# First stream column loaded ahead of the last conditioning weights, and conditioning units moved along the stream of a hybrid decoder step

## The chip, the cores and the metric

The kernel runs on one core of one Trainium2 chip. The metric is the device time of one execution in microseconds (us). Three runs of the kernel before took 1305.91, 1309.7 and 1313.38 us; their median is 1309.7 us.

## What is computed

One layer of a decoder, for 512 prompt rows and 8 single sample rows of width 1024, all in f32:

```python
mod = (c @ w_ada + b_ada)[:, None, :]                 # conditioning: 9 vectors c -> 6 * 1024 columns
sh1, sc1, gt1, sh2, sc2, gt2 = jnp.split(mod, N_MOD, axis=-1)
h = _rmsnorm(x, norm1_g) * (1.0 + sc1) + sh1
proj = h @ w_in                                       # 8768 columns for both mixers
...                                                   # A) sparse attention on q, k, v; B) gated delta rule
mixed = (gate_a * o_nsa + gate_b * o_dn) @ w_out
x = x + gt1 * mixed
h = _rmsnorm(x, norm2_g) * (1.0 + sc2) + sh2
x = x + gt2 * (jnp.square(jax.nn.relu(h @ w_up)) @ w_down)
```

In mixer B a chunk of 128 rows needs the inverse of a triangular matrix per head (the triangular stage), and then a recurrence goes over the four chunks: each chunk's state comes out of the one before. The outputs are the new rows, the caches and the states.

## The kernel before

All work is put into the queues of the engines by one Python program; a scheduling pass then orders each engine's instructions with a simulated timeline, in which work with a higher priority goes first when it is ready. On the chip every engine runs its own list in order and waits on semaphores.

**Conditioning.** `c @ w_ada` is cut into 24 units of 256 columns (`ada`, line 256). A unit has two loads of 512 KB (`ada_load`, line 245, issued by SyncE), 16 matmuls in four row groups into a bank `ek` (line 169), a copy `ma` on ScalarE (line 261), a second small product (line 266, recorded under line 153) and an add on VectorE (line 267). The first 8 units, for the first norm, run at the start (lines 767 to 784): `fetch(n)` issues the loads of the units up to n, seven are issued by the time that j is 3, and the eighth at j = 4. Of their loads all but two go into the pool `q4`, and two into the ring `wraw` of four buffers (`NRAW`). The list `starts` chains these loads: each is issued after the one before it on SyncE.

**Stream.** Everything else that multiplies by weights is a list of units, each 128 columns of `w_in`, later of `w_out`, `w_up` and `w_down`. A unit's weights (`w_load`, line 348, 512 KB, the ring `wraw` again) are split into a rounded part `wh` (ScalarE, line 397, or VectorE, line 399, by kind) and a rest `wl` (VectorE, line 401), and three products are summed (line 153): 48 matmuls in two halves of the rows, each half in one of two banks `pg`. The input is split likewise into `hh` and `hl` by `modulate` (lines 308 to 336), which gives the input in four quarters of two blocks each; a quarter needs two conditioning units. `load_upto` issues loads in the order of the list, about two units ahead; the first stream column is issued by `load_upto(0)` at line 785, chained behind the last of `starts`.

The units' order is written out by hand: the columns for the compressed keys, the gates and mixer B (lines 724 to 734), and then the string `FILL` (line 37), in which `a` is one of the other 16 conditioning units, `q` a query column, `ks` and `kw` two key columns each, `ma` and `mb` the merge gates and `z` the output gate of mixer B. A conditioning unit of `FILL` has both its loads in the ring `wraw`. A `q` may be put down only when the recurrence has finished a chunk (`gate`); its result goes where the triangular matrices `LU` were.

**What runs beside it.** Generators for the triangular stage (`triangular`), the recurrence, the sample rows and the attention put their instructions down between the stream's units, at due times counted in TensorE time of the stream (`run`, line 474), with a higher priority. The last part of the triangular stage is a sequence of small matmuls (32 and 64 wide) with evictions by VectorE and ScalarE. The recurrence begins with `pre1` (line 1139): a scaled transposed key and the decay matrix, whose operand `grhs` is made on VectorE and ScalarE (lines 1001 and 999), multiplied on TensorE and put through an exponential (line 1004). `pre2` (line 1151) is the next product. The sample rows' convolution state `sr` is loaded in eight pieces on ScalarE's queue (line 1286). In the attention the value products use the banks `ek` too (line 1500).

Of the kernel before, what the change touches and what calls it, by code (L numbers as in the profile page):

```python
# [33 lines left out]
ON_B = "vector"  # L34
ON_A = "vector"
WLP = 0
FILL = "a a a a a q ks a a q q kw q a q q q ma ma ma q a z mb a ma z mb ma z mb a z ma mb a ma z a mb ma z a mb a a z z mb mb"
R1 = 5
R2 = 10
R3 = 6.4  # L40
# [29 lines left out]
def hybrid_step(ctx: ExitStack, tc: tile.TileContext, A, O, dbg=None):  # L70


    nc = tc.nc
# [19 lines left out]
    def kb4(pool, shape, dt, name, tag, bufs=None):  # L93
        x = pool.tile([128, 2 * SLOT], dt, name=name, tag=tag, **({} if bufs is None else dict(bufs=bufs)))
        n = 1
        for v in shape:
            n *= v
        x = x[:, 0:n]
        return x if len(shape) == 1 else x.rearrange("p (a b) -> p a b", a=shape[0])
# [79 lines left out]
    for hf in range(2):  # L179
        c = slice(hf * 512, hf * 512 + 512)  # L180
        nc.sync.dma_start(crow[hf][0:1], A["c_prompt"][:, c])
        starts = [nc.sync.dma_start(crow[hf][1:9], A["c_sample"][:, c])]
# [62 lines left out]
    def ada_load(j0, hf, pool=None):  # L245
        if pool is None:
            wa = kb4(wp, (4, 256,), F32, "wa", "wraw", bufs=NRAW)
        else:
            wa = kb4(pool, (4, 256,), F32, "wa", "q4")
        with tc.issue_after(starts[-1].ins) if len(starts) < 17 else nullcontext():  # L250
            r = nc.sync.dma_start(wa, w_ada[:, hf * 4:hf * 4 + 4, j0 * 256:j0 * 256 + 256])
        if len(starts) < 17:
            starts.append(r)
        return wa

    def ada(j0, wa):

        pa = bank("ek")
        quarters(pa[:, 0:256], lambda j, s: cT[:, 18 * j + 9 * s:18 * j + 9 * s + 32], lambda j, s: wa[j // 2][:, j % 2 * 2 + s], True, True, 2)
        ma = e2("ma")[:, 0:256]  # L260
        nc.scalar.copy(out=ma, in_=pa[:, 0:256])

        def rest():
            pt = bank("ek")
            for hf in range(2):
                mm(pt[:, hf * 16:hf * 16 + 9], ma[:, hf * 128:hf * 128 + 128], sel, start=True, stop=True)
            nc.vector.tensor_tensor(mod[:, 2 * j0:2 * j0 + 2], pt[:, 0:32].rearrange("p (b n) -> p b n", b=2)[:, :, 0:9],  # L267
                                    vec[:, 16 + 2 * j0:18 + 2 * j0, None].to_broadcast([128, 2, 9]), op=ALU.add)
        return rest
# [27 lines left out]
    def norm1(t):  # L297
        n = x_rows(t)[1]
        xt = x_tile(t)
        nc.vector.tensor_scalar(xt[0:n], xt[0:n], ssq[0:n, t:t + 1], None, op0=ALU.mult)  # L300
        for hf in range(2):
            x_transposed(xnT, xt[:, hf * 512:(hf + 1) * 512], t, hf * 4, "sc" if hf else "pt")
# [38 lines left out]
    pos = {"unit": 0, "half": 0, "split": 0, "load": 0}  # L341
# [6 lines left out]
    def w_load(ap):  # L348
        def load():
            raw = kb4(wp, (KT, 128,), F32, "raw", "wraw", bufs=NRAW)  # L350
            nc.sync.dma_start(raw, ap)
            return raw
        return load

# [18 lines left out]
    def load_upto(g):  # L373
        while pos["load"] <= min(g, len(groups) - 1):
            x = groups[pos["load"]]
            with tc.issue_after(starts[-1].ins) if pos["load"] == 0 else nullcontext():
                x.raw = x.load()
            pos["load"] += 1

    def split_upto(u):  # L380
        while pos["split"] <= u and pos["split"] < len(units):
            un = units[pos["split"]]
            if "ada" in un and pos["split"] > pos["unit"]:
                return
            load_upto(un["g"])
            if un.get("same"):
                un["w"] = un["same"]["w"]
            elif "ada" not in un:
                raw = groups[un["g"]].raw
                if un.get("keep"):  # L390
                    wh, wl = (kb4(wp, (KT, 128,), F32R, "wk", "wkeep", bufs=NKEEP) for _ in range(2))
                else:
                    wh = kb4(wp, (KT, 128,), F32R, "wh", "wh")
                    wl = kb4(wp, (KT, 128,), F32R, "wl", "wl")
                if un["on"] == "scalar":
                    with tc.issue_after(slot["mixed"].ins) if un.get("keep") else nullcontext():
                        nc.scalar.copy(out=wh, in_=raw)  # L397
                else:
                    (nc.vector if un["on"] == "vector" else nc.gpsimd).tensor_copy(wh, raw)
                kp = KT - WLP  # L400
                nc.vector.tensor_tensor(wl[:, 0:kp], raw[:, 0:kp], f32(wh[:, 0:kp]), op=ALU.subtract)  # L401
                if WLP:
                    nc.gpsimd.tensor_tensor(wl[:, kp:], raw[:, kp:], f32(wh[:, kp:]), op=ALU.subtract)
                un["w"] = wh, wl
                load_upto(un["g"] + 2)
            pos["split"] += 1
# [9 lines left out]
    def step():  # L416
# [7 lines left out]
        if "ada" in un:  # L424
            split_upto(pos["unit"])
            rest = ada(un["ada"], [x.raw for x in groups[un["g"] - 1:un["g"] + 1]])
            load_upto(un["g"] + 2)

            def ev():
                yield  # L430
                yield
                rest()
            e = ev()
            next(e)
            live.append(("ada", e))
            pos["unit"] += 1
            if pos["unit"] < len(units):
                split_upto(pos["unit"])
            return True
# [306 lines left out]
    nxt = {"a": 8, "q": 0, "ma": 0, "z": 0, "mb": 0}  # L746
    for x in FILL.split():
        if x in nxt:
# [11 lines left out]
    def fetch(n):  # L760

        for j in range(len(was), n):
            i = j // 2 + 4 * (j % 2)
            was[i] = [ada_load(i, 0, q4), ada_load(i, 1, None if j % 4 == 3 else q4)]
# [4 lines left out]
    for j in range(8):  # L769
        if j < 5:  # L770
            norm1(j)
        i = j // 2 + 4 * (j % 2)
        rest.append(ada(i, was[i]))
        fetch(j + 4 if j < 5 else 8)
        if j % 2:
            for r in rest:
                r()
            rest = []
            if j < 4:
                continue  # L780
            for i in range(j // 2 if j > 5 else 0, j // 2 + 1):
                modulate(xnT, 0, 0, 8, hh, hl, 2 * i, 2 * i + 2)
            if j == 5:
                slot["early"] = slot["rest"]
# [1215 lines left out]
```

## Time and profile before

| | |
|---|---|
| median of three runs | 1309.7 us |
| the profiled execution | 1307.84 us |
| its span, first to last instruction | 1306.1 us |
| mean granted TensorE clock | 0.969 |
| TensorE, VectorE, ScalarE, GpSimd busy | 93%, 65%, 50%, 18% |
| DMA | 149.82 MB, mean 115 GB/s |

The engines are PE (TensorE), PEld (its weight loads), DVE (VectorE), ACT (ScalarE), POOL (GpSimd) and SP (SyncE); a q behind the name is its queue of DMA issues. A timeline row has the start, the duration, the engine, the line, the operation, the tiles (out, then in) and the count, and in brackets how long the engine was idle before and what ended that. Line 153 is the helper through which nearly all matmuls go, so the tile names tell them apart: `bpg` is the stream, `bek` and `bsp` are the other banks. Most of the span belongs to the stream; the conditioning stands at the start, ahead of the recurrence near 350 us, and in single units up to 812 us.

### The profile page before, as it was taken

To read this page: it belongs to the slowest core of one execution; us is meant where nothing else is said; L and a number is where in the kernel's file an instruction comes from. 1 tells how busy PE (TensorE), PEld (TensorE's weight loads), DVE (VectorE), ACT (ScalarE), POOL (GpSimd) and SP (SyncE) were. 2 spreads that over 40 slices of the span, in tenths; PEclk is the share of its full clock that TensorE was granted. 3 is DMA by queue.
4 is the path that set the end of the run, shared out by engine and by line. 5 is a ranking of instruction groups with operands and counts; after the bars stand their busy time and mean duration, and the time that the engine had idled before them with its cause. 6 is when DMAs were issued, how large, how long until landed. Compare 5 with 4: busy or idle time off the path is not lost. (4 is left out here: it accounts for less than half of the span.)

```text
span 1306.1 us, 26716 instructions
## 1 busy us (share of the span) xinstructions
PE 1216.6 (93%) x10356; PEld 1150.1 (88%) x10356; DVE 843.8 (65%) x2291; ACT 647.2 (50%) x1561; POOL 230.1 (18%) x323
## 2 busy tenths in 40 slices
PE   4899899999888999799998899999999999999997
PEld 3788889989788999678887798989999999999996
DVE  4576958795357788787777787896834334334355
ACT  4565857654243336656646677574643132232244
POOL 2112100112111111312221323230431021020000
PEclk9899989999699999899999899999999999999999
DMA  8852412425613345346344222371732332332533
GB/s 273 216 156 74 126 32 51 119 78 151 182 47 108 103 130 146 98 116 197 99 116 136 74 72 85 94 196 33 210 95 69 98 95 83 97 97 83 161 90 105
DMA packets 234834, 149.82 MB, mean 115 GB/s; under 512 B 9290, under 2 KB 230018, under 8 KB 234444
## 3 DMA queue, kind: packets, MB, share of 16 engines
q1 hardware_dynamic: 224804, 134.77, 36.4%
q0 software_dynamic: 2240, 6.38, 1.8%
q10 hardware_dynamic: 7664, 6.97, 1.8%
q8 instruction: 81, 1.33, 0.4%
q14 instruction: 45, 0.37, 0.1%
HBM read 136.87 MB, written 15.60 MB: 117 GB/s over the span
## 5 line engine op out<-in xcount | busy, mean ns | idle before, releaser
L153 PE MATMUL bpg<-hh,wh 128*128 128x256 f32 (+1 forms) x1168 | 342.2, 293 | 1.2 <-ACT hh L1521 0.7
L153 PE MATMUL bpg<-hh,wl 128*128 128x256 f32 (+1 forms) x1168 | 337.5, 289 | 2.0 <-DVE wl L401 2.0
L153 PE MATMUL bpg<-hl,wh 128*128 128x256 f32 (+1 forms) x1168 | 337.7, 289 | 0.0
L153 PEld LDWEIGHTS bpg<-hh,wh 128*128 128x128 f32 x1168 | 225.2, 193 | 5.2 <-issue 2.0
L153 PEld LDWEIGHTS bpg<-hh,wl 128*128 128x128 f32 x1168 | 224.5, 192 | 4.0 <-DVE wl L401 2.5
L153 PEld LDWEIGHTS bpg<-hl,wh 128*128 128x128 f32 x1168 | 225.5, 193 | 1.5 <-issue 0.8
L401 DVE TENSOR_TENSOR wl<-raw,wh 128x1024 fp32r<-128x1024 f32 x149 | 183.0, 1229 | 65.7 <-ACT wh L397 60.3
L397 ACT CAST wh<-raw 128x1024 fp32r<-128x1024 f32 x117 | 121.6, 1048 | 181.9 <-PE bpg L153 174.5
L153 PE MATMUL bpg<-act,wh 128*128 128x264 f32 (+1 forms) x1024 | 186.5, 284 | 0.0
L153 PEld LDWEIGHTS bpg<-act,wh 128*128 128x128 f32 x1024 | 157.7, 188 | 0.1
L153 PE MATMUL bpg<-act,wl 128*128 128x264 f32 (+1 forms) x512 | 145.0, 284 | 0.2 <-DVE wl L401 0.2
L153 PE MATMUL bpg<-h2h,wh 128*128 128x256 f32 (+1 forms) x448 | 126.7, 283 | 0.0
L153 PE MATMUL bpg<-h2h,wl 128*128 128x256 f32 (+1 forms) x448 | 126.6, 282 | 0.0
L153 PE MATMUL bpg<-h2l,wh 128*128 128x256 f32 (+1 forms) x448 | 126.3, 282 | 0.0
L1848 POOL TENSOR_TENSOR r<-r 128x520 f32<-128x520 f32 (+2 forms) x40 | 54.1, 1354 | 291.2 <-ACT r L1847 291.2
L1811 DVE SCALAR_TENSOR_TENSOR o_dn<-bpg,consts,o_dn 128x256 f32<-128x256 f32 x80 | 38.3, 484 | 100.3 <-PE bpg L153 100.3
L153 PEld LDWEIGHTS bpg<-act,wl 128*128 128x128 f32 x512 | 96.5, 189 | 0.5 <-DVE wl L401 0.4
L153 PEld LDWEIGHTS bpg<-h2h,wl 128*128 128x128 f32 x448 | 84.4, 188 | 0.3 <-DVE wl L401 0.2
L153 PEld LDWEIGHTS bpg<-h2l,wh 128*128 128x128 f32 x448 | 84.4, 188 | 0.0
L153 PEld LDWEIGHTS bpg<-h2h,wh 128*128 128x128 f32 x448 | 84.3, 188 | 0.0
L153 PE MATMUL bsp<-K,qst 128*128 128x288 f32 (+6 forms) x288 | 68.9, 317 | 5.5 <-DVE consts L267 2.3
L1851 DVE TENSOR_TENSOR act<-r,act 128x520 fp32r<-128x520 f32 (+2 forms) x40 | 23.6, 590 | 73.4 <-ACT act L1850 73.3
(634 smaller groups left out, 2453.3 us busy)
## 6 DMA issues: line engine op xcount, KB each, us to landing
raw<-in_w_in SPq DMA_DIRECT2D x68, 512.0 KB
wa<-in_w_ada SPq DMA_DIRECT2D x48, 512.0 KB
raw<-in_w_down SPq DMA_DIRECT2D x40, 512.0 KB
raw<-in_w_up SPq DMA_DIRECT2D x36, 512.0 KB
raw<-in_w_out SPq DMA_DIRECT2D x12, 512.0 KB
Sx<-in_state_dn SPq DMA_DIRECT2D x16, 256.0 KB
out_s_dn<-Sx SPq DMA_DIRECT2D x16, 256.0 KB
pg<-in_cache_k_slc SPq DMA_DIRECT2D x16, 128.0 KB
```

Source lines behind the costliest of these rows:

```text
L153: nc.tensor.matmul(out, lhs, rhs, start=start, stop=stop)
L397: nc.scalar.copy(out=wh, in_=raw)
L401: nc.vector.tensor_tensor(wl[:, 0:kp], raw[:, 0:kp], f32(wh[:, 0:kp]), op=ALU.subtract)
L1811: nc.vector.scalar_tensor_tensor(xi[:, q], p[:, 0:n], mod[:, m + i, 0:1], xi[:, q], op0=ALU.mult, op1=ALU.add)
L1848: nc.gpsimd.tensor_tensor(r, r, r, op=ALU.mult)
L1851: nc.vector.tensor_tensor(b_, r, f32(a), op=ALU.subtract)
```

## The change

It has two parts. The first stream column is issued by `load_upto(0)` when j is 3, that is behind the fourteenth conditioning load and ahead of the last two, and it is a link of the chain `starts`, so that the last two are issued after it. In `FILL` three conditioning units move: five units ahead of the first `q` become three, two behind `ks` become one, and the three come again behind the sixth `q`, behind the third `mb` and, with the last ones spread, between the last `z`.

```diff
--- before.py
+++ after.py
@@ -34,7 +34,7 @@
 ON_B = "vector"
 ON_A = "vector"
 WLP = 0
-FILL = "a a a a a q ks a a q q kw q a q q q ma ma ma q a z mb a ma z mb ma z mb a z ma mb a ma z a mb ma z a mb a a z z mb mb"
+FILL = "a a a q ks a q q kw q a q q q a ma ma ma q a z mb a ma z mb a ma z mb a z ma mb a ma z a mb ma z a mb a z a z a mb mb"
 R1 = 5
 R2 = 10
 R3 = 6.4
@@ -348,7 +348,10 @@
     def w_load(ap):
         def load():
             raw = kb4(wp, (KT, 128,), F32, "raw", "wraw", bufs=NRAW)
-            nc.sync.dma_start(raw, ap)
+            with tc.issue_after(starts[-1].ins) if pos["load"] == 0 else nullcontext():
+                r = nc.sync.dma_start(raw, ap)
+            if pos["load"] == 0:
+                starts[-1] = r
             return raw
         return load
 
@@ -373,8 +376,7 @@
     def load_upto(g):
         while pos["load"] <= min(g, len(groups) - 1):
             x = groups[pos["load"]]
-            with tc.issue_after(starts[-1].ins) if pos["load"] == 0 else nullcontext():
-                x.raw = x.load()
+            x.raw = x.load()
             pos["load"] += 1
 
     def split_upto(u):
@@ -772,6 +774,8 @@
         i = j // 2 + 4 * (j % 2)
         rest.append(ada(i, was[i]))
         fetch(j + 4 if j < 5 else 8)
+        if j == 3:
+            load_upto(0)
         if j % 2:
             for r in rest:
                 r()
```

## Rows read from the trace of the kernel before

**Rows 1.** The page, part 1: busy time, share of the span, instructions.

```profile
PE 1216.6 (93%) x10356; PEld 1150.1 (88%) x10356; DVE 843.8 (65%) x2291; ACT 647.2 (50%) x1561; POOL 230.1 (18%) x323
```

**Rows 2.** The chain that ended last, its longest piece: start, us, what.

```profile
946.57 303.91 PE bpg L153 x2529
```

**Rows 3.** Windows of 25 us: busy PE, PEld, DVE, ACT, POOL; clock; DMA share; GB/s.

```profile
350.00:375.00 25.00, 18.86 (x120) 18.07 (x120) 12.84 (x32) 7.42 (x20) 2.77 (x3) 0.80 0.57 161
...
400.00:425.00 25.00, 25.00 (x237) 22.96 (x237) 20.45 (x54) 8.76 (x22) 2.66 (x2) 1.00 0.54 148
...
725.00:750.00 25.00, 19.75 (x130) 16.95 (x129) 17.63 (x62) 17.57 (x51) 7.98 (x18) 0.80 0.24 65
```

**Rows 4.** Windows ahead of the recurrence, columns as above.

```profile
336.00:342.00 6.00, 6.00 (x131) 5.29 (x130) 2.68 (x6) 0.59 (x1) 0.00 (x0) 0.50 0.49 166
...
349.60:353.60 4.00, 0.02 (x4) 0.03 (x1) 3.33 (x6) 2.96 (x8) 0.00 (x0) 0.77 0.71 164
...
353.60:358.00 4.40, 4.40 (x18) 4.21 (x19) 0.84 (x2) 0.60 (x1) 1.28 (x1) 0.50 1.05 347
```

**Rows 5.** Timeline of the start, several engines: start, us, engine, line, operation, [idle before <-releaser].

```profile
32.95 4.01 SPq L351 DMA_DIRECT2D raw<-in_w_in  x2
...
35.85 1.07 PE L169 MATMUL bek<-wa,consts 128*32 128x256 f32 x16 [1.10 <-DMA wa<-in_w_ada]
...
39.82 1.94 PE L169 MATMUL bek<-wa,consts 128*32 128x256 f32 x16 [2.90 <-DMA wa<-in_w_ada]
...
42.10 1.05 ACT L397 CAST wh<-raw 128x1024 fp32r<-128x1024 f32 x1
...
43.41 0.56 PE L153 MATMUL bpg<-hh,wh 128*128 128x256 f32 x1
...
48.26 0.17 DVE L336 TENSOR_TENSOR hl<-xnT,hh 128x16 fp32r<-128x16 f32 x1
```

**Rows 6.** Timeline of PE ahead of and into the recurrence.

```profile
341.34 1.94 PE L169 MATMUL bek<-wa,consts 128*32 128x256 f32 x16
...
347.15 1.14 PE L153 MATMUL bsp<-iv,TA 64*64 64x64 f32 x30
...
348.54 1.07 PE L169 MATMUL bek<-wa,consts 128*32 128x256 f32 x16
...
353.60 1.19 PE L153 MATMUL bsp<-grhs,rounded 128*128 128x512 f32 x2 [3.98 <-DVE consts L267]
...
354.59 0.41 PE L153 MATMUL bpg<-hh,wh 128*128 128x256 f32 x1
...
356.72 0.86 PE L153 MATMUL bek<-consts,ma 128*128 128x9 f32 x4
...
365.77 0.41 PE L153 MATMUL bsp<-qT,kT 128*128 128x128 f32 x2
```

**Rows 7.** Timeline of SP's queue in the same stretch.

```profile
327.26 0.92 SPq L251 DMA_DIRECT2D wa<-in_w_ada  x2
...
343.30 6.46 SPq L351 DMA_DIRECT2D raw<-in_w_in  x3
```

**Rows 8.** Timelines of DVE and ACT in the same stretch.

```profile
347.41 0.69 DVE L399 CAST wh<-raw 128x1024 fp32r<-128x1024 f32 x1 [4.93 <-DMA raw<-in_w_in]
...
349.12 1.04 ACT L397 CAST wh<-raw 128x1024 fp32r<-128x1024 f32 x1 [3.31 <-DMA raw<-in_w_in]
...
352.77 0.68 DVE L1001 TENSOR_TENSOR grhs<-rounded,gsp 128x512 fp32r<-128x512 f32 x1
...
354.83 7.61 ACTq L1286 DMA_DIRECT2D sr<-in_state_conv  x8
```

**Rows 9.** Timeline of PE later: a conditioning unit, its second product, a wait.

```profile
411.90 1.07 PE L169 MATMUL bek<-wa,consts 128*32 128x256 f32 x16
...
423.05 0.51 PE L153 MATMUL bek<-consts,ma 128*128 128x9 f32 x4
...
735.56 0.50 PE L153 MATMUL bsp<-K,qst 128*128 128x288 f32 x2 [2.28 <-DVE consts L267]
```

## The prediction

> **What bounds the kernel now.** I read the page's table of engines first. TensorE is busy for 93% of the span, VectorE for 65%, ScalarE for 50% [rows 1]. The chain of waits, followed back from the end, is 303.91 us of TensorE without a break from 946.57 us on: 2529 matmuls, 0.12 us each [rows 2]. So whatever reaches that point earlier ends earlier by as much, and the question is only when TensorE gets there. The table by windows shows where it loses time before that: 18.86 of 25 us busy at 350 to 375 at a clock of 0.80, 25.00 of 25 at 400 to 425, 19.75 of 25 at 725 to 750 [rows 3]. The loss at 350 is the place that the change touches. Inside it TensorE does next to nothing for 4.0 us (349.60 to 353.60), and then runs at a granted clock of 0.50, that is 1.2 GHz, from 353.60 [rows 4]. The timelines of the single engines tell why.
>
> **Part one, the load order at the start.** Three weight columns matter here. In the kernel before, SyncE issues the first two stream columns at 32.95, after all sixteen loads of the first eight conditioning units [rows 5]. The matmuls of the seventh unit's last load begin at 35.85, those of the eighth at 39.82, and both waited for their loads, so two loads of 512 KB take 39.82 - 35.85 = 3.97, about 2.0 us each. The first column is cast from 42.10, the second follows, and the stream begins at 43.41 [rows 5]. The change puts the first column ahead of the last two conditioning loads, issues no DMA more, and passes no other queue. So the column lands about 4 us earlier, and each of the two loads that it passes 2.0 us later.
> What this is worth: TensorE stands idle from 36.92 (35.85 + 1.07) to 39.82, 2.90 us. At best the cast begins at 42.10 - 3.97 = 38.13, its 1.05 us end at 39.2, and stream matmuls fill the gap 0.6 us before the eighth unit would have begun: -0.6. At worst TensorE's queue still has the eighth unit first, and all behind it is 2.0 us later: +2.0. The eighth unit also feeds the last quarter of the normalised input, whose last piece is written at 48.26, 4.85 us after the stream begins [rows 5]; that piece gets later too, while the 36 matmuls that don't need it take between 36 x 0.12 = 4.3 us and, at the doubled step of the slow clock, 8.6 us, so they cover it nearly. Between -0.6 and +2.0 I take 0: the row nearest to the deciding one is the 2.90 us gap, which is there either way, and the work on TensorE is the same.
>
> **Part two, two conditioning units fewer ahead of the recurrence.** Five units stand there before (the fourth begins at 341.34, the fifth at 348.54), three after. Their weights share a ring of four buffers with the stream columns, so the columns behind them are issued only as the units free buffers: the three columns after the five units go out at 343.30, right after the fourth unit (341.34 + 1.94 = 343.28) [rows 6, 7]. They land late: VectorE waits 4.93 us for one until 347.41, ScalarE 3.31 us for the next until 349.12, and both engines are in order, so what the recurrence's first decay product needs stands behind these casts and is made only at 352.77 + 0.68 = 353.45 [rows 8]. TensorE begins that product at 353.60 after 3.98 us idle, and the page's name for the releaser, a conditioning add, is only the piece that came last [rows 6].
> After the change the ring holds the columns two units earlier in its order. The load pair that goes out at 327.26 [rows 7], when the second unit is through, is then the first two of these three columns. Landing as late after issue as before (347.41 - 343.30 = 4.1), they are there at 331.4, long before the casts are due. So the wait of 3.98 us goes, and so does the work of the two units, 1.94 and 1.07. Both ends: if only the wait goes, -4.0; if TensorE runs straight on from its last small matmul (347.15 + 1.14 = 348.29), the two units gone as well, -(3.98 + 1.94 + 1.07) = -7.0. Late next is the eviction of these small matmuls on VectorE and ScalarE, in order ahead of the decay operand; it will take some of it back. I take the middle, **-5.5**.
> Behind that product nothing more is gained. The next recurrence product begins at 365.77, and ahead of it stand transposes of a small state whose eight loads ScalarE issues from 354.83 for 7.61 us, right behind the decay's exponential [rows 6, 8]. That chain moves as a whole with the product at 353.60. The stream column that runs beside it from 354.59 at the slow clock (18 matmuls of all kinds in 4.40 us [rows 4]), and the two small conditioning products (0.86 us at 356.72 is one of two) are hidden under it: 0. It could be -2 if the state's loads gain by having fewer weight loads beside them, DMA share 1.05 there [rows 4], or +1.
> The Trainium skill, Perfetto Trace Analysis, section Matmul Optimizations, speaks against this: the matmul engine scales with its use, so matmuls should run back to back, and the two units did fill the triangular stage. The row says that they don't keep the clock up: at 336 to 342 TensorE is busy 6.00 of 6.00 us and is granted 0.50 [rows 4]. By the rule the sum would be that of the clock rival below; by the row it stays.
>
> **Part three, where the units go.** Behind the recurrence's first columns stood two units, the first at 411.90; now there is one. A unit costs 1.07 plus 0.51 for its second product [rows 9], 1.6 us at full clock. TensorE is full there (25.00 of 25 [rows 3]), so -1.6. Further on, in the attention stretch, three units come in: +4.8 if TensorE is full at each, 0 if each falls into idle time. The nearest rows point both ways, 25.00 and 19.75 busy of 25 [rows 3]; as most of the stretch is full I take the full +4.8. Their loads go out two units ahead as all others do, and no unit there waited for its weights.
> Sum: 0 - 5.5 + 0 - 1.6 + 4.8 = -2.3. The profiled execution took 1307.84 (span 1306.1 and 1.7 around it), so 1305.5, which I round to **1306**. The median shown is 1309.7, 1.9 above the profiled execution, and the lowest run is 1305.91; the forecast is for a median near the profiled run.
>
> **Rivals.**
> *The late units are hidden* (chance 0.27). Part two is worth 5.5 to 7.0, the 1.6 comes off, and the three units fall into gaps of the attention: -7.1 to -8.6, with the state's loads -10.6, so 1297 to 1301. For it: 5.25 us idle at 725 to 750. Against: 400 to 425 is full.
> *The wait stays* (0.08): the column loads are emitted at another place, the casts wait as before, and only the unit's 1.94 goes: -1.9 - 1.6 + 4.8 = +1.3, 1309. Against it is the ring's order.
> *The clock* (0.05): the front stays at 1.2 GHz until the second column. That costs the 48 matmuls of the first column some 0.10 us each at most: -2.3 + 4.8 = +2.5, 1310.
> *The late units hold the attention up* (0.14, slower). The accumulation banks of a conditioning unit are the two that the attention's value products use. At 735.56 TensorE waited 2.28 us with a conditioning add as releaser [rows 9], and that stretch lost 5.25 us in all. Three more such places at 1.6 + 5.25 each are +20.6 at the most; with -5.5 - 1.6 and the start's +2.0 it would be 1323, and at 1.6 + 2.28 each +4.5, 1312. It decides from about 4.4 us a unit, where the gain of 7.1 and 6 more are eaten; I put it at 1315 as a whole, since two of the three will hardly meet the worst stretch. Against it: most units of this stretch show no such wait.
>
> **How the numbers follow.** Forecast 0.46, the rivals as above. A measurement of this kernel can tell about 0.5%, 6.5 us, from no change. Faster by more is the second case, 0.27; within are forecast, staying wait and clock, 0.46 + 0.08 + 0.05 = 0.59; slower 0.14. The forecast's own range is 1303 to 1309 (-7.0 or -4.0 in part two in place of -5.5, the start's -0.6 to +2.0 in place of 0). The range that should hold 8 in 10 reaches to 1297 on the hidden side, and to 1314 on the other, leaving the worst third or so of the slow rival and the runs' own scatter outside.
>
> **What would show it.** Right: no cast of a stream column waits for its load just before the recurrence, the decay product begins 4 to 7 us earlier, the stream begins within 2 us of 43.41, and three units more stand behind 470 us. Wrong in part two: a wait for a column load again ahead of the decay product, or the next product not moved with it. Wrong in part three: TensorE's idle time between 400 and 900 grown by more than 5 us, or shrunk by as much. The whole is wrong if the planner that orders the queues gives the stream another order far from the edits.

## The result, and the profile after

The kernel after takes 1322.68 us (median of 11 runs, 1318.52 to 1327.7), the kernel before 1314.03 us (11 runs, 1305.91 to 1316.61): a ratio of 1.007, 95% interval 1.0048 to 1.0093. It is slower, by some 9 us; 1306 us had been forecast. Over more runs the kernel before stands 4 us above the median of three that was shown at first, and its profiled execution (1307.84 us) was one of its quickest, so a part of every difference between the two traces is that one execution's luck. A control below gives a size for it.

The page of the kernel after, part 1, against [rows 1]:

```profile
PE 1227.0 (93%) x10356; PEld 1158.6 (88%) x10356; DVE 843.5 (64%) x2291; ACT 649.7 (49%) x1561; POOL 227.9 (17%) x323
```

The work is the same: 10356 matmuls before and after, and no other engine is busier by more than 3 us. TensorE is busy 10.4 us longer for them, and its idle time went from 1306.1 - 1216.6 = 89.5 to 1320.2 - 1227.0 = 93.2 us. So three quarters of the 14.1 us between the two traces are not idle time but longer work on the same matmuls. The mean granted clock is 0.962 after and 0.969 before. An estimate from these, with 1.2 and 2.4 GHz as the two levels: 2 x 0.038 x 1320.2 = 100 us at the lower level after, 2 x 0.031 x 1306.1 = 81 before, and half of the 19 us between them is 10 us. The longest piece of the chain that ended last answers [rows 2]:

```profile
960.92 303.42 PE bpg L153 x2528
```

The piece is as long as before and starts 14.35 us later. The whole difference of the two spans (1320.2 - 1306.1 = 14.1) is thus there before 961 us, as the prediction's first paragraph had it; it is the way up to there that came out otherwise.

The start of the kernel after, timelines of SP, PE and DVE, against [rows 5]:

```profile
32.34 0.50 SPq L352 DMA_DIRECT2D raw<-in_w_in  x1
32.93 2.38 SPq L251 DMA_DIRECT2D wa<-in_w_ada  x2
...
36.79 1.93 PE L169 MATMUL bek<-wa,consts 128*32 128x256 f32 x16 [1.56 <-DMA wa<-in_w_ada]
40.67 0.58 PE L153 MATMUL bpg<-hh,wh 128*128 128x256 f32 x1 [1.94 <-ACT wh L399]
...
41.83 1.94 PE L169 MATMUL bek<-wa,consts 128*32 128x256 f32 x16
43.70 1.03 PE L153 MATMUL bek<-consts,ma 128*128 128x9 f32 x4
...
48.58 0.85 PE L153 MATMUL bek<-consts,ma 128*128 128x9 f32 x4
...
52.32 0.17 DVE L336 TENSOR_TENSOR hl<-xnT,hh 128x16 fp32r<-128x16 f32 x1
```

The column does pass the last two conditioning loads. The eighth unit begins 2.0 us later (41.83), as worked out; the stream begins 2.7 us earlier (40.67), which is less than the 4.2 us of the prediction's best case (39.2) and more than the 2 us that it named as the sign of being right. What had not been worked out stands in the last three rows: of the eighth and seventh unit's small second products one group begins at 43.70, the other only at 48.58, behind eighteen stream matmuls that step 0.21 us, at the slow clock. So the last piece of the input comes at 52.32, 4.06 us later than before, where the prediction had it nearly covered.

The front of the recurrence, PE of the kernel after, against [rows 6]:

```profile
337.60 1.93 PE L169 MATMUL bek<-wa,consts 128*32 128x256 f32 x16
...
348.53 0.56 PE L153 MATMUL bpg<-hh,wh 128*128 128x256 f32 x1
...
351.24 0.41 PE L153 MATMUL bpg<-hh,wh 128*128 128x256 f32 x1
...
355.41 1.14 PE L153 MATMUL bsp<-iv,TA 64*64 64x64 f32 x30
...
357.88 0.62 PE L153 MATMUL bsp<-grhs,rounded 128*128 128x512 f32 x2
...
364.93 1.13 PE L153 MATMUL bsp<-qT,kT 128*128 128x128 f32 x8 [0.27 <-DVE scy L1309]
```

Two units are gone, and the wait of 3.98 us ahead of the decay product is gone with them. But the product begins at 357.88, 4.3 us later than before, where the whole program is already 4.9 us behind (by so much the copy of the conditioning unit at 325 us is later). It gained 0.6 us. Thirteen stream matmuls from 348.53 to 351.24 took the units' place ahead of the small matmuls (`iv,TA`), which end at 356.55 instead of 348.29. The gain comes behind the product: 7.05 us to the next recurrence product (364.93 - 357.88) instead of 12.17, so that this one is 0.8 us earlier than before in spite of the lag, a gain of 5.7.

Two casts still wait for their loads, but 18 to 20 us ahead of the product in place of 4 to 6; DVE and ACT of the kernel after, against [rows 8]:

```profile
337.58 1.16 DVE L401 CAST wh<-raw 128x1024 fp32r<-128x1024 f32 x1 [3.44 <-DMA raw<-in_w_in]
...
339.52 1.05 ACT L399 CAST wh<-raw 128x1024 fp32r<-128x1024 f32 x1 [2.75 <-DMA raw<-in_w_in]
```

Two new waits stand further on, PE of the kernel after (at the second key column of the window's keys, and at the end of the attention), and the windows around the first:

```profile
466.42 0.58 PE L153 MATMUL bpg<-hh,wh 128*128 128x256 f32 x1 [3.87 <-ACT kvt L498]
...
875.83 0.80 PE L153 MATMUL bpg<-hh,wh 128*128 128x256 f32 x2 [4.00 <-ACT hh L1525]
```

```profile
460.00:465.00 5.00, 2.54 (x27) 2.25 (x20) 4.92 (x13) 2.12 (x6) 0.00 (x0) 1.00 0.40 117
465.00:470.00 5.00, 3.58 (x17) 3.59 (x18) 2.61 (x7) 1.27 (x3) 1.01 (x1) 0.57 0.09 26
470.00:475.00 5.00, 5.00 (x33) 4.78 (x33) 1.12 (x7) 1.84 (x4) 1.28 (x1) 0.75 0.00 0
475.00:480.00 5.00, 5.00 (x44) 4.96 (x43) 2.74 (x9) 0.66 (x2) 0.00 (x0) 1.00 0.19 56
```

The copy `kvt` waits for a buffer whose content is still being stored (ACT of the kernel after):

```profile
465.99 0.65 ACT L498 COPY kvt<-bpg 128x256 f32<-128x256 f32 x2 [2.90 <-DMA out_p_k_win<-kst]
```

TensorE stands idle 3.87 us, and the mean clock granted in the two windows from 465 on is 0.57, close to the lower level (0.50, 1.2 GHz), and 0.75: 77 matmuls from 460 to 475 where full windows have some 48 in five. The Trainium skill, Perfetto Trace Analysis, section Matmul Optimizations, says that the engine scales with its use, so that matmuls should run back to back. At this place the trace agrees, 1.00 in the window of the gap and 0.57 in the one behind it.

### The profile page after: what moved, and what is told of

Its sections match the earlier page's. It is cut to its first block, busy times and chain, and to the rows that moved or that the text cites. A ratio compares the mean times of both kernels' runs of the same rounds, so it can differ in the third digit from the quotient of the medians.

```text
span 1320.2 us, 26709 instructions
## 1 busy us (share of the span) xinstructions
PE 1227.0 (93%) x10356; PEld 1158.6 (88%) x10356; DVE 843.5 (64%) x2291; ACT 649.7 (49%) x1561; POOL 227.9 (17%) x323
## 4 chain that ended last, share of the span: by engine, by line
PE 60%; DVE 9%; ACT 3%; DMA 2%; issue 2%; POOL 0%; ACTq 0%; POOLq 0%; DVEq 0%; SPq 0%
PE bpg L153 44%; PE bsp L153 7%; PE bsp L160 4%; PE bek L153 3%; PE bek L169 2%; DVE wl L403 1%; ACT ps L1468 1%; DMA raw<-in_w_in 1%; DVE ptl L1500 0%; DVE h2l L332 0%; DVE h L330 0%; PE bsp L169 0%; DVE ps L1444 0%; PE bek L160 0%; DVE Sx L1404 0%
## 5 line engine op out<-in xcount | busy, mean ns | idle before, releaser
L153 PE MATMUL bpg<-hh,wh 128*128 128x264 f32 (+1 forms) x1168 | 346.1, 297 | 10.2 <-ACT hh L1525 4.0
L153 PE MATMUL bpg<-hh,wl 128*128 128x264 f32 (+1 forms) x1168 | 340.0, 292 | 2.7 <-DVE wl L403 2.7
L153 PE MATMUL bpg<-hl,wh 128*128 128x264 f32 (+1 forms) x1168 | 340.5, 292 | 0.0
L153 PEld LDWEIGHTS bpg<-hh,wh 128*128 128x128 f32 x1168 | 228.6, 196 | 15.5 <-ACT hh L1525 4.3
L153 PEld LDWEIGHTS bpg<-hh,wl 128*128 128x128 f32 x1168 | 227.3, 195 | 5.2 <-DVE wl L403 3.4
L153 PEld LDWEIGHTS bpg<-hl,wh 128*128 128x128 f32 x1168 | 228.6, 196 | 2.1 <-issue 1.2
L1852 POOL TENSOR_TENSOR r<-r 128x520 f32<-128x520 f32 (+2 forms) x40 | 51.2, 1281 | 294.6 <-ACT r L1851 294.5
L153 PE MATMUL bsp<-K,qst 128*128 128x256 f32 (+6 forms) x288 | 67.7, 318 | 2.4 <-DVE mx L1444 1.0
```

The source lines that it names most:

```text
L153: nc.tensor.matmul(out, lhs, rhs, start=start, stop=stop)
L1852: nc.gpsimd.tensor_tensor(r, r, r, op=ALU.mult)
```

## The experiments

All ratios are to the kernel before on the same chip, with 95% intervals; 1% is 13.1 us. The last column counts the lines taken out of and put into a listing of TensorE's instructions in their order (some 7400 lines, like ones in a row together), against that of before: an edit makes the scheduling pass order anew. Rows of the traces, counted in the same way, give 1481 for the change, 296 for e6 and 10 for e9, so these counts hold to some tens of lines.

| run | edit | ratio | interval | us | order lines |
|---|---|---|---|---|---|
| after | the change | 1.0070 | 1.0048 to 1.0093 | +9.2 | 1520 |
| e9 | control, same order | 0.9997 | 0.9978 to 1.0016 | -0.4 | 0 |
| e6 | one front unit moved | 0.9962 | 0.9942 to 0.9981 | -5.0 | 238 |
| e7 | late units spread another way | 1.0024 | 1.0006 to 1.0042 | +3.1 | 322 |
| e16 | e6 with e5 | 0.9978 | 0.9957 to 1.0000 | -2.9 | 448 |
| e14 | before, other ring | 1.0060 | 1.0034 to 1.0085 | +7.9 | 855 |
| e8 | unit behind ks moved, end spread | 1.0155 | 1.0126 to 1.0184 | +20 | 939 |
| e5 | e2, start held | 1.0011 | 0.9996 to 1.0026 | +1.4 | 957 |
| e2 | load order alone | 1.0076 | 1.0049 to 1.0102 | +10 | 968 |
| e15 | load order, double | 1.0060 | 1.0034 to 1.0087 | +7.9 | 1123 |
| e4 | before, kst elsewhere | 1.0212 | 1.0181 to 1.0242 | +28 | 1214 |
| e1 | FILL alone | 1.0027 | 1.0005 to 1.0049 | +3.5 | 1233 |
| e12 | after, both mended | 1.0073 | 1.0046 to 1.0100 | +9.6 | 1449 |
| e11 | after, end mended | 1.0074 | 1.0047 to 1.0101 | +9.7 | 1470 |
| e10 | after, start held | 1.0092 | 1.0065 to 1.0119 | +12 | 1513 |
| e13 | after, other ring | 1.0093 | 1.0068 to 1.0117 | +12 | 1543 |
| e3 | after, kst elsewhere | 1.0180 | 1.0150 to 1.0210 | +24 | 1641 |

**The two halves (e1, e2).** e1 has the new `FILL` with the old load order, e2 the new load order with the old `FILL`.

> The order string of the change with the load order of before. Theory A (two separate losses: the eighth conditioning unit later at the start, and a stall of the recurrence on a key store): faster than the change by the start's 2 to 5 us, so +4 to +7 us over before, with the decay product 5 us early and the stall in the k_win unit still there. Theory B (the load order alone is to blame): 0 to -5 us against before. Theory C (any new order of the planner moves the time by several us): no relation to either, and no stall at the same place.

> The load order of the change with the order string of before. Theory A: +2 to +5 us over before, the loss seen at the first 65 us and kept. Theory B: +7 to +10, the whole loss. Theory C: anything between -8 and +8, with the loss or gain arising far from the start.

The load order alone, priced at 0, costs 10 us (6.4 to 13.4). `FILL`, forecast at -2.3, costs 3.5 (0.7 to 6.4). Their sum, 13.5 (some 9 to 18), can't be told from the change's 9.2 (6.3 to 12.2). Theories A and B both fail in e1: its decay product begins at 353.80 (353.60 before), the wait of `kvt` is not in its trace, and the time is above B's.

**The key store's buffer (e3, e4).** The ring of four in which `kvt` and `kst` take turns is left to the others, and `kst` gets its buffers from another:

```diff
-    wk = ctx.enter_context(tc.tile_pool(name="wk", bufs=10))
+    wk = ctx.enter_context(tc.tile_pool(name="wk", bufs=9))
-        st = v4(e2("kst")[:, 0:512]) if st is None else st()
+        st = v4(t2("kst")[:, 0:512]) if st is None else st()
```

> The change, with the staging tile of the key stores taken from the pool of 2 KB scratch tiles in place of the four buffers it shares with the copies of the stream's results; that pool has nine buffers in place of ten, to make it fit. Theory A: the wait of ScalarE's copy for the store of the first k_win half (2.9 us, TensorE 3.87 us idle and 9 us at half clock behind it) goes, and the kernel is 6 to 9 us faster than the change, +0 to +3 over before. If the stall is only where a deficit shows that exists anyway: within 2 us of the change. Theory C: unrelated.

> The control for e3: the same two edits on the kernel before, where no copy of this stretch waits for a store. Theory A: within 3 us of before. Theory C: several us off although nothing that it touches was waited for.

The wait of `kvt` is gone from e3, and e3 is the slowest version with the change. But the edit costs the kernel before 28 us, so the pair says nothing of the wait. Whether nine buffers of the other ring in place of ten cost this, or the order written anew, no run separates.

**The start held (e5).** e2, and the first stream unit's matmuls (line 453 of before) issued behind the eighth unit's second product:

```diff
+            with tc.issue_after(slot8["last"].ins) if pos["unit"] == 0 else nullcontext():
+                mm(p_, wh[:, k], xh[:, k, c], start=(k == 0), stop=False)
...
```

> The load order of the kernel after with FILL of before (as in e2), and the first stream unit's matmuls (L453 to 455 of before) held behind the eighth unit's second product, so that TensorE's order at the start is that of before again while the column still lands first. If the interleaving at the start is what costs (twenty stream matmuls at the low clock between the two products of the eighth unit, last hl piece at 52.32 instead of 48.26), the last hl piece is back at 48 to 49, the lag at the stream's 65 us is under 0.7 us, and the time is 1.000 to 1.003 of before (+0 to +4 us) against 1.0076 in e2. If the whole loss comes from the order written out further down, which differs from that of before in some 950 lines on TensorE as it does in e2, it stays at 1.005 to 1.009 although the start is mended. If the column's earlier transfer itself holds the eighth unit up, the start lags by 0.6 to 2 us still and the time is 1.003 to 1.006.

The last `hl` piece is at 49.68 and the time at 1.0011: of e2's 10 us, 8.6 are back (the difference of the ratios is 0.65% with an interval of 0.35 to 0.95%). By this run alone the interleaving at the start would be the cause. But in the trace of e5 the lag of the first stage is not gone; ACT of before, of e2 and of e5 at the triangular stage's first decay:

```profile
198.17 0.60 ACT L1004 ACTIVATE dcy<-bsp 128x512 f32<-128x512 f32 x1 [0.60 <-PE bsp L153]
...
203.41 0.60 ACT L1008 ACTIVATE dcy<-bsp 128x512 f32<-128x512 f32 x1
...
203.61 0.60 ACT L1012 ACTIVATE dcy<-bsp 128x512 f32<-128x512 f32 x1 [1.41 <-PE bsp L153]
```

The gain appears between there and the attention's end: the last value product begins 14.6 us later than before in e2 (901.58 against 887.00) and 5.2 in e5 (892.23).

**One piece of FILL at a time (e6, e7, e8).** The strings, cut to what differs:

```
before  a a a a a q ks a a q q kw q a q q q ma ...
e6      a a a a q ks a a q q kw q a q q q a ma ...
before  ... a ma z a mb ma z a mb a a z z mb mb
e7      ... a ma z a mb ma z mb z a z a a mb mb
before  a a a a a q ks a a q q kw ... ma z a mb a a z z mb mb
e8      a a a a a q ks a q q kw ... ma z a mb a z a z a mb mb
```

> Before, with one conditioning unit alone taken from the front of FILL and put behind the sixth q; load order of before, and the written order differs little (238 lines on TensorE against 1233 in e1). Theory of the prediction: the unit's price falls away ahead of the recurrence and its raw loads come 1.5 us or more earlier, so the first at of the recurrence comes 2 to 3.5 us earlier than before (367.2), and the unit's 1.6 us are paid back behind it: time 0.998 to 1.000 of before (-2.5 to 0 us). Rival (any re-planned order costs): the first at earlier by the same, but the time 1.001 to 1.004. Rival (the wait stays): first at within 0.7 us of before, time 1.000 to 1.001.

> Before, with only the last conditioning units of FILL spread as in the kernel after (no unit leaves the front; two late units are moved behind other units): load order of before. Everything up to the recurrence should stand within 0.5 us of before. Theory of the prediction: a late unit costs its 1.6 us wherever it stands, so nothing: time within 0.999 to 1.001. Rival (late units hold the attention up, because the products of a unit fall into waits of its own copies): 1.002 to 1.004, with the lag appearing behind 700 us.

> Before, with only the third conditioning unit (behind ks) moved to the end of FILL: load order of before, the order written out differs much (939 lines on TensorE). Theory of the prediction: 1.6 us gained at its place and 1.6 us paid back at the end: time 0.999 to 1.001. Theory of the scatter of the written order: a time outside of 0.998 to 1.002, with lags and gains at places that the unit does not touch (compression at 150 to 175 us, attention).

In `e6` the unit goes behind the seventh `q` (as in the change, where the other two go behind the second `mb` and to the end; the section on the change says sixth and third). e6 gains 5.0 us (2.5 to 7.6): of the versions tried it is the only one that beats the kernel before by more than the noise, 1307.63 us beside 1313.05 on the same chip. The gain was not seen where it was expected: in its trace the first `at` of the recurrence (line 1155, its product times the decay, on VectorE) begins at 370.94, 3.7 us later than before, where 2 to 3.5 earlier had been forecast. e7 loses 3.1 where 0 was forecast, and PE of e7 shows the same wait as the kernel after at the attention's end:

```profile
864.84 0.79 PE L153 MATMUL bpg<-hh,wh 128*128 128x256 f32 x2 [4.21 <-ACT hh L1521]
```

Before, that wait is 0.7 us. e8 loses 20 us for one unit of 1.6, with the wait of `kvt` (3.8 us) and that of `hh` (4.1 us) both in it; they don't make up 20. The end of e7 is spread in another way than that of the change, so e7 is no piece of it; e8 has the change's own end. e6 and e8 add to +15, and e1, which holds both and moves one front unit more, has +3.5: unless that unit is worth -12, the pieces don't add.

**The control (e9).** Before, with the column's load asked for at another place in the code that leaves every queue as it was (`if j == 4: load_upto(0)`).

> Before, with the first stream column's load asked for one step of the starting loop earlier in the code (L774 to 776), where it still stands behind the last conditioning load on SP: the order on each engine and queue is that of before, instruction by instruction. A control: the time should be 0.9985 to 1.0015 of before. Its trace is a second execution of the same order; if its milestones (eighth unit's weights, first decay near 198, first at near 367, first attention value near 540) differ from those of before by under 1 us, differences of 2 to 5 us between the traces of two kernels can be read; if they differ by 2 to 5 us, those can't, and only the timed rounds and named waits count.

No difference in time. Its trace is a second execution of the same order, and it is instructive; PE of e9, against [rows 6]:

```profile
348.50 1.94 PE L169 MATMUL bek<-wa,consts 128*32 128x256 f32 x16
350.80 1.19 PE L153 MATMUL bsp<-grhs,rounded 128*128 128x512 f32 x2 [0.37 <-DVE consts L267]
...
361.48 1.08 PE L153 MATMUL bsp<-qT,kT 128*128 128x128 f32 x8
```

The wait of 3.98 us on which part two rested is 0.37 here. The product has not come nearer by that: it stands 28.1 us behind the copy of the conditioning unit at 325 us in both executions (350.80 - 322.67 and 353.60 - 325.42). The engine was at work for longer, the fifth unit at 348.50 for 1.94 us in place of 1.07. The wait is no accident either: of the nine traces with five units ahead of the first `q` seven have 3.3 to 4.3 us there, and of the nine with fewer none has any. The first decay is 2.7 us earlier than in the other execution, the next recurrence product 4.3, the first attention value 1.5, and at the end it is 1.1 us behind. So a difference of up to 4 us at one place of two traces may be nothing. Measured like the kernel after, e9 gains 4.3 - 2.75 = 1.5 us between the conditioning unit at 325 and the next recurrence product without any change; of part two's 5.7 in the kernel after some 4 remain beside that. All traces together bear this out: that stretch takes 34.6 to 36.5 us in six of the seven with the new front of `FILL` (29.2 in e3) and 38.0 to 43.2 in the eleven others.

**Mending the change (e10, e11, e12).** e10 is after with e5's edit; e11 has the end of `FILL` as `a a a z z mb mb`; e12 has both.

> The kernel after, with the first stream unit's matmuls held behind the eighth conditioning unit's second product, as in e5. If the interleaving at the start is what the load order costs in the whole change as well, the time falls from 1.007 to that of FILL alone (e1, 1.0027), within 1.001 to 1.005, and the last hl piece comes at 49 to 50 instead of 52.3. If the order written further down decides, it may be anywhere from 1.000 to 1.015, with the k_win copy's wait (3.9 us at L498 of after) there or not.

> The kernel after, with the end of FILL written as a a a z z mb mb instead of a z a z a mb mb, so that the last two z units again stand behind the last conditioning unit, as before. If the 4.0 us for which TensorE waits on hh (L1525) at the end of attention come from the z units being used up too early, that wait falls under 1.5 us and the time to 1.003 to 1.005 of before (3 to 5 us under the kernel after). If the last units' places don't matter (each unit its 1.6 us, as the prediction has it), the time stays at 1.006 to 1.008.

> The kernel after with both edits, e10's and e11's. If the two losses are separate and add, the time is that of e10 less 3 to 5 us, near 0.998 to 1.001 of before, that is the -2.3 us that the prediction gave to parts two and three. If the written order's scatter decides, it lies outside of that, and no sum over the two edits gives it.

In e11 the wait on `hh` is gone from PE's waits, and the trace is 4.4 us shorter (1315.8), but the timed runs don't show it: 1.0074 against 1.0070. The intervals together leave room for 4 us either way. Holding the start, worth 8.6 us alone, gives nothing here (1.0092, with the last `hl` piece at 50.94): that difference between e5 and e10 is beyond the intervals. e12, whose trace has neither the wait on `hh` nor that of `kvt`, stands at 1.0073, where 0.998 to 1.001 was expected if the two losses add.

**The wait of kvt (e13, e14).** The `vbd` tiles come from the other ring, and e14 is the same in before:

```diff
-            r = [v4(e2("vbd", F32R)[0:72, 0:512]) for _ in range(2)]
+            r = [v4(t2("vbd", F32R)[0:72, 0:512]) for _ in range(2)]
```

> The kernel after, with the two vbd tiles of each recurrence step (L1396) taken from the ring t2k in place of e2k, so that k_win's copy (L498) no longer comes round to the buffer whose store has just been issued. Theory: the copy's 2.9 us and TensorE's 3.9 us behind it at 462 to 466 us go; first to last at of the recurrence, 113.6 us in after against 104.7 before and 108.3 in e1, falls to 104 to 109; and the time falls by 4 to 8 us against the kernel after, to 1.001 to 1.004 of before. Rival (the order written anew moves the time by as much as any single wait): the wait goes, but the time lies anywhere from 0.998 to 1.02.

> The kernel before with the same edit: its control. Before has no such wait, so by the theory of the wait nothing is gained: 0.999 to 1.002. By the rival the new order alone makes it anything from 0.998 to 1.02 (moving kst out of the ring, e4, made it 1.021).

The wait goes, and the place is mended; windows of e13, against those of the kernel after above:

```profile
460.00:465.00 5.00, 5.00 (x55) 4.66 (x55) 4.84 (x11) 3.51 (x10) 0.00 (x0) 1.00 0.16 49
465.00:470.00 5.00, 5.00 (x48) 4.72 (x50) 4.32 (x11) 0.70 (x2) 1.01 (x1) 1.00 0.57 164
470.00:475.00 5.00, 5.00 (x48) 4.44 (x41) 4.59 (x11) 1.81 (x4) 1.85 (x1) 1.00 0.62 201
```

151 matmuls where the kernel after had 77, at full clock. Yet the time is 1.0093, and before with the same edit, which had no such wait to lose, is 7.9 us slower. So this wait is real and dear where it stands, and it does not decide the time. It was expected to bring the kernel to 1.001 to 1.004, and the stretch from the first to the last `at` from 113.5 us to 104 to 109; that fails, the stretch takes 112.3. Where else the time went, in an order written anew, was not traced.

**Double dose, and a sum (e15, e16).** e15 puts the column ahead of the last four conditioning loads (`if j == 2`), e16 has e6's `FILL` with e5's loads and hold.

> FILL of before, with the first stream column's load put ahead of the last four conditioning loads instead of the last two (dose of e2). If the loss of e2 (1.0076) is the conditioning units' later weights, it doubles: the eighth unit's weights land 1.5 us or more later than in e2, the last hl piece comes at 53 to 56 us, and the time is 1.010 to 1.016. If it is the order written anew, there is no dose: 0.998 to 1.02, not tied to the start's lag.

> e6's one front unit moved, together with e5's load order and held first unit. If the effects of edits add, 0.9962 + 0.0011 = 0.997 (0.995 to 0.999); if each order is its own draw, outside of that.

In e15 the eighth unit begins 5.5 us later than before, more than twice as late as in the kernel after; PE of e15, and ACT of e15 and of e9 at the triangular stage's first decay:

```profile
45.37 1.07 PE L169 MATMUL bek<-wa,consts 128*32 128x256 f32 x16
```

```profile
197.72 0.60 ACT L1008 ACTIVATE dcy<-bsp 128x512 f32<-128x512 f32 x1 [0.49 <-PE bsp L153]
...
195.43 0.60 ACT L1008 ACTIVATE dcy<-bsp 128x512 f32<-128x512 f32 x1 [0.60 <-PE bsp L153]
```

The kernel before has that decay at 198.17 in one execution and 195.43 in the other (e9). So most of the start's delay is taken back by 198 us, if not all, and the larger part of the 7.9 us is lost behind it: the first `at` of the recurrence is at 366.79 (before 367.19, e9 363.53), the last at 476.78 (471.88, 470.65), and the last value product is 8.7 us later than before.

That is e15 alone: over the traces the five with the change's load order and no hold have the last piece of the input at 51.2 to 52.5 and the first decay at 199.3 to 203.9, the eight with the old load order 47.4 to 50.1 and 194.3 to 200.2. So the change's start does lag by some 5 us there on average; e5, with the same lag, ends at +1.4, so the lag does not decide the end.

A dose is not seen: 1.006 with two loads passed by more than in e2, 1.0076 in e2, and the last `hl` piece at 51.52 instead of 53 to 56. e16 came within its expected sum (0.9978, 0.9957 to 1.0000), although one of its two edits rewrites 957 lines alone; these two do add, as far as this can tell.

## Why the prediction was wrong

Of the 17 us between 1305.5 and 1322.68, 6.2 are the level from which the forecast started (1307.84, where 11 runs have a median of 1314.03); the other 11 are the change, forecast at -2.3 and measured at +8.7 between the medians.

**Part one** was priced at 0 with bounds of -0.6 to +2.0, and it is the term that failed by most: the edit costs 10 us alone (e2), and inside the change still 5.6 (1.0070 against 1.0027, 0.1 to 0.75% by the intervals). At the start itself the loads moved as worked out, the stream earlier and the eighth unit 2.0 us later; but TensorE put eighteen stream matmuls at the slow clock between the small second products, the last piece of the input came 4.06 us later, and the first decay some 5, beyond the bound of +2.0. That this lag is not what is paid at the end, e5 shows (same lag, +1.4); that the rest is the cost of the order that the pass wrote after the loads is argued, not shown.

**Part two**, -5.5, came out at its place as -3.8 (e1: 4.9 us earlier, of which 1.1 stood before) to -5.7 (after) between the traces, 2 to 4 beside e9. The mechanism was half wrong: the wait went, but the decay product gained 0.6 us (over all the traces nothing: it stands 27.0 to 28.7 us behind that copy with five units ahead, 27.3 to 29.5 with three, e3 aside), since stream matmuls were put where the units had been, and the rest came behind it, where 0 had been taken. That the size was nearly right is luck. The recurrence then takes the gain back: from its first to its last `at` it needs 104.7 us before, 107.1 in e9 and 113.5 after. No run shows why; e13 without the wait of `kvt` still needs 112.3, and of all traces the ten with both units behind `ks` have 104.7 to 110.4, the eight with one 108.3 to 115.2.

**Part three**, -1.6 + 4.8, is wrong in its first figure above all: to take the unit behind `ks` away was to gain 1.6 and, with the unit put down at the end, to cost nothing; e8 has +20. The late units, a price for each wherever it stands, cost 3.1 us by being spread alone, in e7's way. A wait on the last pieces of the attention comes with the spread end, and goes with it in e11; that it is what costs is not shown, as e11 is not faster.

**The rivals.** None was borne out. *The late units hold the attention up* gave 1312 to 1323 and comes nearest by the number, but TensorE's idle time from 480 to 900 is 29.1 us after (420 - 390.94) and 29.5 before (420 - 390.46). *The clock* looked only ahead of the recurrence, at +2.5 us; the lower clock came at 465 us and in other places, 10 us of busy time in all between the two traces. The two rows behind that, windows of before and of after:

```profile
480.00:900.00 420.00, 390.46 (x3189) 355.56 (x3189) 331.07 (x1099) 258.40 (x758) 100.38 (x199) 0.97 0.41 117
```

```profile
480.00:900.00 420.00, 390.94 (x3197) 353.49 (x3196) 334.51 (x1105) 261.41 (x760) 102.13 (x200) 0.96 0.43 127
```

**The step that failed** is one that the prediction wrote down last and gave no chance: "The whole is wrong if the planner that orders the queues gives the stream another order far from the edits." It did, in 1520 lines of TensorE's list. The sum added local prices over an order, and a clock, taken as fixed. What the runs show: every edit with more than 800 lines of difference lost time, from +1.4 (e5, not to be told from 0) to +28 us, whatever it was meant to do; those under 450 lay between -5.0 and +3.1. Within the first group the count prices nothing: 939 lines cost 20 us in e8, 957 cost 1.4 in e5. The 9 us have no single place that was found. Single waits could be found and removed, 3.9 us at `kvt` and 4.0 us at `hh`, and in e12 both, and the time did not follow.

**What stays open.** Which trait of the rewritten orders costs the time is not settled. That before's order is a good draw among many, so that nearly any other is worse, fits all the runs, but it was argued and not shown: no run has kept all of before's order under the new load order, or let only the order change. How an order costs, by more idle time or by a lower clock, differs too; the 18 traces show both. TensorE's busy time for the same 10356 matmuls runs from 1216.6 to 1243.1 us and follows the mean granted clock (correlation -0.92), and its idle time runs from 86.1 (e6) to 100.0 us (e8).

## What to carry to other kernels

Where a pass orders the queues, compare the orders first: an edit that rewrites a tenth of a list is not priced by what it moves, and its range must be that of a new order, here +1 to +28 us. Take edits singly, and look for those that leave the order nearly alone; one front unit (238 lines) brought 5.0 us, three units with a load (1520 lines) lost 9. And take a second trace of the same kernel before building on one wait: 3.98 us was 0.37 in the next execution, and the product behind it came no sooner for that.

## What the runs showed that was not expected

One order's own scatter goes with the clock: over 29 executions of the kernel before on one chip the span has a mean of 1311.1 us, a standard deviation of 3.3 us, and falls by 0.79 us for each 0.001 of the mean granted clock (correlation -0.86). The profiled execution, at 0.969, was at the quick end, so the two traces differ by 14.1 us where the medians differ by 8.7. Between two orders the clock takes a share that is not the same: the 12 runs of e1 were granted 0.9595 on average and the 23 of the kernel before beside them 0.9643, which at the 0.99 us for each 0.001 that these 23 show is 4.7 us, all that e1 loses; e15 was granted 0.9649 beside 0.9645, and none of its loss is the clock's.

A delay of the first stage need not reach the end: in e15 5.5 us at 45 us had become -0.4 us at 198 beside the one execution of before, and 2.3 beside the other. And a wait in a full stretch costs more than its own length: 3.87 us of idle time at 466 us left TensorE with 77 matmuls in 15 us, where e13 without it had 151.
